# Selecting per-head decays with strips of 32 rows, and applying them to products that two heads share

## The chip, the cores and the metric

The kernel runs on one core of one Trainium2 chip. The metric is device time in microseconds (us) for one execution, the median of three runs. The core has a matrix engine (TensorE, PE in the profile; its weight loads stand apart as PEld), a vector engine (VectorE, DVE), a scalar engine (ScalarE, ACT), GpSimd (POOL), and DMA queues issued here mostly by SyncE (SP). Matmul results land in PSUM, which this kernel hands out in eight banks of 128 partitions by 512 floats.

## The reference

A four-layer model on 256 latent tokens that read 256 context tokens, width 1024. Layers 0 and 3 mix tokens with a bidirectional state-space scan (SSD), layer 1 with spatial gating, layer 2 with retention; each is followed by a SwiGLU FFN. The change lies in the SSD layers alone. Cut to what matters, for each of 32 heads of 64 channels, in each direction, over chunks of 128 tokens:

```
cum    = cumsum(a)                               # a = dt * A, one number per token and head
y      = (C B^T * exp(cum_i - cum_j), masked) @ v        # within the chunk
y     += (C @ state) * exp(cum)                  # from earlier chunks
state  = state * exp(cum[-1]) + B^T @ (v * exp(cum[-1] - cum))
y_all  = y_forward + y_backward + d_skip * x
```

C and B (128 numbers per token) are common to the eight heads of a group; the decays differ by head. Layer 0 computes 512 tokens (four chunks), layer 3 needs outputs for the 256 latent tokens only, with the context's final states still carried in.

## The kernel before

Channels lie on partitions and tokens along the free dimension. Projections are three matmuls per 128x128 weight tile (`mm3`, L306 to L308): the f32 operands are split into a rounded part and a remainder, declared float32r. A stream of weight tiles comes in over SP's queue and is split two ways, `whi` by ACT (L226) and `wlo` by DVE (L227), three units ahead of use.

The order is written by hand. `run` walks the projection jobs of a group of heads, and after each job emits the next slot from a list made by `scan_slots`. A slot holds steps of head pairs (four pairs for each of four groups, so 16 per SSD layer):

- `T_` transposes a pair's inputs (L998), ACT copies them out (L1000), and DVE weights them four times (L1006) into `vs` and `vo`.
- `V_` forms the context states `S` (L1019); ACT copies and POOL multiplies them (L1023, L1025).
- `A_` broadcasts the cumulative decays `ER` of one head over 128 partitions by a matmul with a selector column of `SEL` (L1041, L1049); DVE multiplies them into each head's own operands: `SO` (L1043, L1051) and `C2` (L1053).
- `K_` does the same with the log decays `FR`, on top of a mask: for each head and direction one bfloat16 matmul `IDB` by `NEG` (L1063) and one selector matmul (L1065) into the same bank. ACT takes 16 exponentials of 128 columns in layer 0, 8 in layer 3 (L1070), and DVE adds directions and multiplies with the scores into `E` (L1071, L1072).
- `Y_` sums, per head and into 64 output partitions, the within-chunk term (`E`), the neighbouring chunk (`SO`) and the carried state (`C2`), all in L1091; DVE adds `d * x` (L1095).

`FR` and `ER` hold 64 rows (direction, head) with rounded parts above and remainders below, made once per layer in `b` of `dt_steps` (emitted as the slot `dtb`), from cumulative sums `p3` of `LA`, which POOL produces (L918). Every `ps()` takes the next of the eight PSUM banks in turn, so the ninth allocation waits for the release of the first. DVE, ACT and POOL execute in emission order.

Of the kernel before, what the change touches and what calls it, by code (L numbers as in the profile page):

```python
# [9 lines left out]
F32 = mybir.dt.float32  # L10
# [102 lines left out]
def backbone(ctx, tc, A, out):  # L113
# [33 lines left out]
    def f32(ap):  # L147
        return ap.bitcast(F32)
# [11 lines left out]
    SEL = cp.tile([P, 64], F32R, name="SEL")  # L160
# [642 lines left out]
    def ssd(i, j, need_ctx, prev_last, prev_ranges, norms, fin_norms):  # L803
# [5 lines left out]
        with ExitStack() as ph:  # L809
# [18 lines left out]
            def prep():  # L828
# [5 lines left out]
                if i == 0:  # L834
                    act.copy(IDB, ident)
                    for d, m in ((0, M_GT), (1, M_LT)):
                        dve.tensor_scalar(NEG[d], m, -2.0 ** 100, None, op0=MUL)
                    act.copy(SEL, CST[:, C_SEL:C_SEL + 64])

# [43 lines left out]
            ER = qt([NTOK], "er", dt=F32R)  # L883
# [3 lines left out]
            def dt_steps():  # L887
# [34 lines left out]
                def b():  # L922
# [16 lines left out]
                    act.copy(FR[:64], p3[:64])  # L939
                    dve.tensor_tensor(FR[64:], p3[:64], f32(FR[:64]), op=SUB)  # L940
                    ef = tmp(512, "th", 2)[:64]
                    act.activation(ef, p3[:64], AF.Exp)
                    act.copy(ER[:64], ef)
                    dve.tensor_tensor(ER[64:], ef, f32(ER[:64]), op=SUB)
# [16 lines left out]
            def scan_slots(g):  # L961
# [26 lines left out]
                def pair(hp):  # L988
# [42 lines left out]
                    def sel(d_, h):  # L1031
                        return SEL[:, 32 * d_ + h:32 * d_ + h + 1].to_broadcast([P, P])

                    def A_():
                        pst["C2"] = qt([2, 2, T], "C2", c2)
                        SO = pst["SO"] = qt([2 * W // T, T], "SO", 2)
                        if need_ctx:
                            pt = ps("g")
                            for hh in range(2):
                                for d_ in range(2):  # L1040
                                    pe.matmul(pt[:, (2 * hh + d_) * P:(2 * hh + d_ + 1) * P], sel(d_, h0 + hh),  # L1041
                                              ER[:, (1 - d_) * P:(2 - d_) * P], start=True, stop=True)
                            dve.tensor_tensor(  # L1043
                                SO[:, 0:2], pt.rearrange("p (h n) -> p h n", h=2),
                                st["SF"][:, 0:1].to_broadcast([P, 2, T]), op=MUL)
                        for hh in range(2):
                            pt = ps("g")
                            for d_ in range(2):
                                pe.matmul(pt[:, d_ * T:(d_ + 1) * T], sel(d_, h0 + hh), ER[:, T:],  # L1049
                                          start=True, stop=True)  # L1050
                            dve.tensor_tensor(SO[:, 2 * W // T - 2 + hh], pt[:, P:3 * P], st["SF"][:, W // T - 1], op=MUL)  # L1051
                            C2 = pst["C2"][:, hh]
                            dve.tensor_tensor(  # L1053
                                C2, pt.rearrange("p (d n) -> p d n", d=2),
                                Cg[:, T:].unsqueeze(1).to_broadcast([P, 2, T]), op=MUL)

                    def K_():
                        for hh in range(2):
                            h = h0 + hh
                            pts = [ps("g") for _ in range(2 * W // 512)]  # L1060
# [836 lines left out]
```

## Time and profile before

| | us |
|---|---|
| median of 3 runs (range) | 2883.96 (2882.82 to 2887.27) |
| the profiled execution | 2887.09 |
| its span in the trace | 2885.3 |
| scan of layer 0, in the trace | about 91 to 484 |
| scan of layer 3, in the trace | about 2395 to 2651 |

Times in the trace count from the start of the span. A row of the timeline gives a start, a length and the merged instructions; matmul lengths include the pipeline's drain, so what one costs in a stream is read from the distance between starts. A float32 matmul appears as two instructions (two passes), a float32r or bfloat16 one as one instruction.

### The profile page before, as it was taken

How to read it: one execution, taken by the hardware profiler on the slowest of the kernel's cores; microseconds unless marked ns; L12 is line 12 of the kernel's file. 1: busy time of each engine (PE TensorE's matmuls, PEld its weight loads, DVE VectorE, ACT ScalarE, POOL GpSimd, SP SyncE). 2: the span in 40 equal slices, each digit the busy share in tenths (PEclk: the TensorE clock that was granted, in tenths of full speed). 3: DMA queues.
4: the chain of work that ended last, by engine and by line, in shares of the span. 5: the costliest groups of instructions: out<-in, count | busy, mean ns of one | idle time of the engine just before them, and what ended most of it. 6: DMA issues, size and time to landing. Idle time of an engine off the chain costs nothing.

```text
span 2885.3 us, 40761 instructions
## 1 busy us (share of the span) xinstructions
PE 2822.3 (98%) x16180; PEld 2392.1 (83%) x16180; DVE 1926.2 (67%) x3150; ACT 1092.8 (38%) x1935; POOL 220.7 (8%) x294
## 2 busy tenths in 40 slices
PE   7999999999999999999999999999999999999998
PEld 5787877888889888988889777779888898888998
DVE  5876767678875266677777344346777779888565
ACT  4455444322224422422224322224322245554443
POOL 0210001200001000100001000001000022101000
PEclk9999999999999999999999999999999999999899
DMA  6322233255543222355443222213555422223454
GB/s 235 107 88 103 88 110 118 103 192 195 197 182 110 95 81 88 114 189 174 174 175 118 80 73 88 77 70 110 184 181 176 172 90 99 100 97 118 151 177 140
DMA packets 111678, 376.37 MB, mean 130 GB/s; under 512 B 12160, under 2 KB 16640, under 8 KB 111488
## 3 DMA queue, kind: packets, MB, share of 16 engines
q1 hardware_dynamic: 109296, 367.23, 36.1%
q0 software_dynamic: 1616, 5.77, 0.6%
q8 instruction: 127, 2.08, 0.3%
q10 hardware_dynamic: 576, 0.77, 0.1%
q14 instruction: 63, 0.52, 0.1%
HBM read 369.53 MB, written 4.19 MB: 130 GB/s over the span
## 4 chain that ended last, share of the span: by engine, by line
PE 83%; DVE 6%; issue 6%; ACT 3%; POOL 2%; DMA 0%; POOLq 0%; DVEq 0%; ACTq 0%; SPq 0%
PE mm L306 24%; PE mm L308 24%; PE mm L307 24%; PE y L1091 2%; DVE wlo L227 1%; PE s L1019 1%; PE g L1448 1%; PE g L1063 1%; PE g L1065 1%; DVE AL L577 1%; ACT whi L226 0%; PE y L1312 0%; PE y L1466 0%; PE y L1465 0%; PE s L500 0%
## 5 line engine op out<-in xcount | busy, mean ns | idle before, releaser
L306 PE MATMUL mm<-AH,whi 128*128 128x512 f32 (+1 forms) x2456 | 889.4, 362 | 2.0 <-ACT AH L590 1.6
L308 PE MATMUL mm<-AH,wlo 128*128 128x512 f32 (+1 forms) x2456 | 878.7, 358 | 0.0
L307 PE MATMUL mm<-AL,whi 128*128 128x512 f32 (+1 forms) x2456 | 876.3, 357 | 0.6 <-DVE AL L1120 0.4
L227 DVE TENSOR_TENSOR wlo<-st,whi 128x1024 fp32r<-128x1024 f32 (+1 forms) x502 | 588.7, 1177 | 317.2 <-ACT whi L226 316.9
L226 ACT CAST whi<-st 128x1024 fp32r<-128x1024 f32 (+1 forms) x502 | 503.7, 1008 | 345.9 <-PE mm L307 216.1
L306 PEld LDWEIGHTS mm<-AH,whi 128*128 128x128 f32 x2456 | 463.3, 189 | 74.4 <-issue 3.6
L307 PEld LDWEIGHTS mm<-AL,whi 128*128 128x128 f32 x2456 | 462.9, 188 | 71.3 <-issue 1.2
L308 PEld LDWEIGHTS mm<-AH,wlo 128*128 128x128 f32 x2456 | 462.7, 188 | 71.5
L412 DVE SCALAR_TENSOR_TENSOR mj<-mst,cb 128x1024 bf16<-128x1024 f32 x304 | 371.2, 1221 | 21.8 <-DMA mst<-in_mod_w_dram 16.3
L611 DVE SCALAR_TENSOR_TENSOR X<-mm,MOD,X 128x256 f32<-128x256 f32 x332 | 148.0, 478 | 95.2 <-PE mm L308 95.0
L306 PE MATMUL mm<-hh,whi 128*128 128x512 f32 (+1 forms) x576 | 209.0, 363 | 0.0
L308 PE MATMUL mm<-hh,wlo 128*128 128x512 f32 (+1 forms) x576 | 209.0, 363 | 0.0
L307 PE MATMUL mm<-hl,whi 128*128 128x512 f32 (+1 forms) x576 | 208.8, 363 | 0.0
L306 PE MATMUL mm<-yg,whi 128*128 128x256 f32 (+1 forms) x592 | 198.5, 335 | 1.0 <-ACT yg L1502 1.0
L307 PE MATMUL mm<-yg,whi 128*128 128x256 f32 (+1 forms) x592 | 191.6, 324 | 0.3 <-DVE yg L1503 0.3
L308 PE MATMUL mm<-yg,wlo 128*128 128x256 f32 (+1 forms) x592 | 191.6, 324 | 0.0
L1591 ACT CAST hh<-s 128x512 fp32r<-128x512 f32 (+1 forms) x72 | 40.8, 567 | 288.5 <-DVE s L1581 288.5
L1581 DVE TENSOR_TENSOR s<-s,mm 128x512 f32<-128x512 f32 (+1 forms) x88 | 54.5, 619 | 124.8 <-PE mm L308 124.8
L1563 ACT ACTIVATE s<-mm 128x512 f32<-128x512 f32 (+1 forms) x88 | 47.9, 544 | 210.8 <-PE mm L308 210.7
L308 PEld LDWEIGHTS mm<-hh,wlo 128*128 128x128 f32 x576 | 108.7, 189 | 17.0
L306 PEld LDWEIGHTS mm<-yg,whi 128*128 128x128 f32 x592 | 112.6, 190 | 12.3 <-issue 1.5
L307 PEld LDWEIGHTS mm<-hl,whi 128*128 128x128 f32 x576 | 108.7, 189 | 16.9
(366 smaller groups left out, 3907.9 us busy)
## 6 DMA issues: line engine op xcount, KB each, us to landing
st<-in_ffn_w_dram SPq DMA_DIRECT2D x176, 512.0 KB, 3.3
mst<-in_mod_w_dram SPq DMA_DIRECT2D x152, 512.0 KB, 4.2
st<-in_ssd_in_dram SPq DMA_DIRECT2D x82, 512.0 KB, 3.3
st<-in_ffn_w2a_dram SPq DMA_DIRECT2D x96, 384.0 KB, 3.0
st<-in_ssd_out_dram SPq DMA_DIRECT2D x32, 512.0 KB, 3.3
st<-in_ret_in_dram SPq DMA_DIRECT2D x32, 512.0 KB, 3.3
st<-in_mod_n_dram SPq DMA_DIRECT2D x24, 512.0 KB, 4.1
st<-in_ffn_w2b_dram SPq DMA_DIRECT2D x16, 512.0 KB, 3.8
```

Source lines behind the costliest of these rows:

```text
L226: act.copy(hi[:, :n], t[:, :n])
L227: dve.tensor_tensor(lo[:, :n], t[:, :n], f32(hi[:, :n]), op=SUB)
L306: pe.matmul(pt, lh, rh, start=(start and i == 0), stop=False)
L307: pe.matmul(pt, lh, rl, start=False, stop=False)
L308: pe.matmul(pt, ll, rh, start=False, stop=(stop and i == n - 1))
L412: dve.scalar_tensor_tensor(j, t, 1.0, mp[1][:, v], op0=MUL, op1=MUL, accum_out=MOD[:, i, v, ct:ct + 1])
L577: dve.scalar_tensor_tensor(AL[:, m, n0:n1], u, sh, f32(AH[:, m, n0:n1]), op0=ADD, op1=SUB)
L611: dve.scalar_tensor_tensor(X[:, m, a:b], pt[:, a - n0:b - n0], g, X[:, m, a:b], op0=MUL, op1=ADD)
L1091: pe.matmul(pt[hs, c * P:(c + 1) * P], l_, r_, start=first[hh], stop=(n_ == len(seq) - 1))
L1563: act.activation(t[:, :b - a], pt, AF.Silu)
L1581: dve.tensor_tensor(s, s, pt, op=MUL)
L1591: act.copy(hh[:, a:b], s)
```

## The change

1. `SEL` shrinks to 16 columns with the same pattern in each strip of 32 rows; a sign column `SGN` marks the rows of remainders.
2. `FR` and `ER` are laid out as four strips of 32 rows: strip 2*direction + head parity, 16 rows of rounded parts and 16 of remainders. For that, DVE copies `LA` into a reordered `la` before the `p3` matmuls, which become 16 instead of 8.
3. `K_` issues the four mask matmuls first, then the four selector matmuls, each of 32 rows by 128 columns in a strip of its own.
4. `A_` selects with tiles of 32 rows by 64 columns, in float32; `er[d]` holds both heads' decays in their 64 partitions each. Beside it `gd[d]` holds both heads' products of state with C and of `vo` with `SF`, 128 wide. ACT copies `er` out, DVE multiplies, POOL adds the directions, and DVE adds `d * x`.
5. `Y_` keeps the within-chunk term only. `SO` and `C2` as operands are gone.
6. `A_` moves from the slot ahead of `K_` to the slot of `K_` behind it (layer 0) or the slot after it (layer 3); `V_` moves with the slots.

```
-    SEL = cp.tile([P, 64], F32R, name="SEL")
+    SEL = cp.tile([P, 16], F32R, name="SEL")
+    SGN = cp.tile([P, 3], F32, name="SGN")
...
+                    la = tmp(512, "th", 2)
+                    dve.tensor_copy(la.rearrange("p (c b k h) -> p c b k h", c=8, b=2, k=2),
+                                    LA.rearrange("p c (d h b) -> p (c d) b h", d=2, b=2).unsqueeze(3)
+                                    .to_broadcast([P, 8, 2, 2, 16]))
                     for k in range(4):
-                        for d_, m in ((0, M_LE), (1, M_GE)):
-                            pe.matmul(p3[32 * d_:32 * d_ + 32, k * P:(k + 1) * P],
-                                      LA[:, k, 32 * d_:32 * d_ + 32], m, start=True, stop=True)
+                        for z, m in enumerate((M_LE, M_LE, M_GE, M_GE)):
+                            pe.matmul(p3[32 * z:32 * z + 32, k * P:(k + 1) * P],
+                                      la[:, P * k + 32 * z:P * k + 32 * z + 32], m, start=True, stop=True)
...
-                    act.copy(FR[:64], p3[:64])
-                    dve.tensor_tensor(FR[64:], p3[:64], f32(FR[:64]), op=SUB)
...
+                    def parts(out, x, t):
+                        act.copy(out, x)
+                        dve.tensor_scalar(t, x, SGN[:, 0:1], None, op0=MUL)
+                        dve.scalar_tensor_tensor(out, f32(out), SGN[:, 1:2], t, op0=MUL, op1=ADD)
+                    parts(FR, p3, tmp(512, "th", 2))
...
                     def A_():
...
+                        o = P if need_ctx else 0
+                        er = [ps("g") for _ in range(2)]
+                        gd = [ps("g") for _ in range(2)]
+                        for a, b, n in (((0, o, P),) if need_ctx else ()) + ((o, o + T, T),):
+                            for d_ in range(2):
+                                c = T if n == T else (1 - d_) * P
+                                for hh in range(2):
+                                    pe.matmul(er[d_][64 * hh:64 * hh + 64, a:b], f32(sel(d_, h0 + hh, 64)),
+                                              ER[rows(d_, h0 + hh), c:c + n], start=True, stop=True)
+                        S, vo, SF = pst["S"], pst["vo"], st["SF"]
+                        for d_ in range(2):
+                            ks = slice(d_ * P, (d_ + 1) * P)
+                            seq = [(o + k * P, S[:, d_, k ^ d_], Cg[:, (2 + k) * P:(3 + k) * P]) for k in range(2)]
+                            seq.append((o + (1 - d_) * P, vo[:, d_, 1], SF[:, W // T - 1, ks]))
+                            if need_ctx:
+                                seq.append((0, vo[:, d_, 0], SF[:, 0, ks]))
+                            for n_, (a, l_, r_) in enumerate(seq):
+                                pe.matmul(gd[d_][:, a:a + P], l_, r_, start=(n_ == 0), stop=(n_ == len(seq) - 1))
+                        U = qt([W], "SO", 2)
+                        ec = qt([3 * T + 2 * o], "C2", c2)
+                        L = ec[:, 2 * (o + T):]
+                        x = XT[ct]
+                        for d_ in range(2):
+                            out = U[:, W - T:] if d_ == 0 else L
+                            sc = ec[:, d_ * (o + T):(d_ + 1) * (o + T)]
+                            act.copy(sc, er[d_][:, :o + T])
+                            if need_ctx and d_ == 0:
+                                dve.tensor_tensor(U[:, P:], gd[0][:, :P + T], sc[:, :P + T], op=MUL)
+                                continue
+                            if need_ctx:
+                                dve.tensor_tensor(U[:, :P], gd[1][:, :P], sc[:, :P], op=MUL)
+                            dve.tensor_tensor(out, gd[d_][:, o:o + T], sc[:, o:o + T], op=MUL)
+                        pool.tensor_tensor(U[:, W - T:], U[:, W - T:], L, op=ADD)
+                        dve.scalar_tensor_tensor(
+                            x[:, lo:], x[:, lo:], prm("ssd_d", j * 16 + ct), U, op0=MUL, op1=ADD)
...
                     def K_():
...
+                                gs[d_, hh] = ps("g")[:, :W]
+                                pe.matmul(gs[d_, hh], IDB, NEG[d_].unsqueeze(1).to_broadcast([P, 4 - c0, P]),
+                                          start=True, stop=False)
+                        for hh in range(2):
+                            for d_ in range(2):
+                                pe.matmul(gs[d_, hh], sel(d_, h0 + hh, P), FR[rows(d_, h0 + hh), lo:],
+                                          start=False, stop=True)
...
-                        dve.scalar_tensor_tensor(
-                            x[:, lo:], x[:, lo:], prm("ssd_d", j * 16 + ct), pt[:, lo:], op0=MUL, op1=ADD)
+                        dve.tensor_tensor(x[:, lo:], pt[:, lo:], x[:, lo:], op=ADD)
...
                 if need_ctx:
                     return [
-                        [init, TT[0]], [AA[0], VV[0]], [KK[0], TT[1]],
-                        [YY[0], AA[1], VV[1]], [KK[1], TT[2]],
-                        [YY[1], AA[2], VV[2]], [KK[2], TT[3]],
-                        [YY[2], AA[3], VV[3]], [KK[3]], [YY[3]]]
+                        [init, TT[0]], [VV[0]], [KK[0], AA[0], TT[1]],
+                        [YY[0], VV[1]], [KK[1], AA[1], TT[2]],
+                        [YY[1], VV[2]], [KK[2], AA[2], TT[3]],
+                        [YY[2], VV[3]], [KK[3], AA[3]], [YY[3]]]
 
                 return [
-                    [init, TT[0]], [AA[0]], [VV[0], KK[0], TT[1]], [AA[1]],
-                    [YY[0], VV[1], KK[1], TT[2]], [AA[2]], [YY[1], VV[2], KK[2], TT[3]], [AA[3]],
-                    [YY[2], VV[3], KK[3]], [], [YY[3]]]
+                    [init, TT[0]], [VV[0]], [KK[0], TT[1]], [AA[0], VV[1]],
+                    [YY[0], KK[1], TT[2]], [AA[1], VV[2]], [YY[1], KK[2], TT[3]], [AA[2], VV[3]],
+                    [YY[2], KK[3]], [AA[3]], [YY[3]]]
```

## Rows read from the trace of the kernel before

**Rows 1.** The page: busy time by engine; the chain that ended last.

```profile
PE 2822.3 (98%) x16180; PEld 2392.1 (83%) x16180; DVE 1926.2 (67%) x3150; ACT 1092.8 (38%) x1935; POOL 220.7 (8%) x294
...
PE 83%; DVE 6%; issue 6%; ACT 3%; POOL 2%; DMA 0%; POOLq 0%; DVEq 0%; ACTq 0%; SPq 0%
```

**Rows 2.** Busy time in the two scans: stretch, length, PE, PEld, DVE, ACT, POOL, clock.

```profile
91.00:484.00 393.00, 388.28 (x2611) 310.27 (x2612) 283.35 (x434) 198.68 (x482) 35.39 (x48) 1.00 0.28 96
2395.00:2651.00 256.00, 253.12 (x2019) 228.22 (x2020) 224.78 (x416) 139.91 (x317) 28.90 (x49) 0.99 0.27 93
```

**Rows 3.** Timeline of PE, layer 0, 186 to 199: start, length, engine, line, operation.

```profile
186.62 1.07 PE L422 MATMUL y<-st,CC 128*32 128x256 f32 x16
187.62 0.50 PE L306 MATMUL mm<-yg,whi 128*128 128x512 f32 x1
...
190.51 0.56 PE L1041 MATMUL g<-er,SEL 128*128 128x128 f32 x4
190.91 0.68 PE L1049 MATMUL g<-er,SEL 128*128 128x256 f32 x4
191.43 1.05 PE L1019 MATMUL s<-vps,btok 128*128 128x128 f32 x8
...
197.80 0.39 PE L1063 MATMUL g<-NEG,IDB 128*128 128x512 bf16 x1
...
198.27 0.39 PE L1063 MATMUL g<-NEG,IDB 128*128 128x512 bf16 x1
```

**Rows 4.** Timeline, layer 0, 118 to 122: the pair's `Y_` between its neighbours.

```profile
118.06 0.39 PE L307 MATMUL mm<-AL,whi 128*128 128x512 f32 x1
...
118.29 0.40 PE L308 MATMUL mm<-AH,wlo 128*128 128x512 f32 x1
...
118.61 1.09 PE L1091 MATMUL y<-E,xtok 128*64 128x128 f32 x16
...
119.54 1.04 PE L1091 MATMUL y<-SO,vpo 128*64 128x128 f32 x16
...
121.38 0.66 PE L1041 MATMUL g<-er,SEL 128*128 128x128 f32 x4
```

**Rows 5.** Timeline of PE, layer 3, 2481 to 2485.

```profile
2481.97 0.61 PE L1091 MATMUL y<-SO,vpo 128*64 128x128 f32 x8
...
2483.38 1.16 PE L1019 MATMUL s<-vps,btok 128*128 128x128 f32 x8
2484.38 0.27 PE L1063 MATMUL g<-NEG,IDB 128*128 128x256 bf16 x1
...
2484.61 0.28 PE L1063 MATMUL g<-NEG,IDB 128*128 128x256 bf16 x1
```

**Rows 6.** Costliest groups, shapes apart: count, busy us, mean ns, idle before.

```profile
L1053 DVE TENSOR_TENSOR C<-g,ct 128x512 f32<-128x512 f32 x64 | 43.4, 678 | 0.0
...
L1196 POOL TENSOR_TENSOR X<-X,AH 128x256 f32<-128x256 f32 x12 | 8.8, 749 | 15.1 <-DVE X L1195 15.1
```

**Rows 7.** Timeline, layer 0, at `dtb`: PE's sums and DVE's queue.

```profile
92.75 1.07 PE L933 MATMUL g<-CST,SF 128*32 128x128 f32 x16
...
93.26 0.67 DVE L1144 SCALAR_TENSOR_TENSOR zt<-zt,mm 128x512 f32<-128x512 f32 x1
```

**Rows 8.** Timeline, layer 3, at `dtb`: the same two.

```profile
2398.81 1.92 PE L933 MATMUL g<-CST,SF 128*32 128x128 f32 x16
...
2399.98 0.41 DVE L1144 SCALAR_TENSOR_TENSOR zt<-zt,mm 128x256 f32<-128x256 f32 x1
```

**Rows 9.** Timeline, end of layer 0's scan: idle before, and what ended it, in brackets.

```profile
464.33 0.75 DVE L1006 TENSOR_TENSOR vps<-xtok,ws 128x256 f32<-128x256 f32 x2
464.56 1.06 PE L1091 MATMUL y<-E,xtok 128*64 128x128 f32 x13 [1.62 <-DVE E L1072]
...
475.32 4.23 ACT L1070 ACTIVATE E<-g,bi 128x128 f32<-128x128 f32 x16
...
481.14 0.95 PE L1091 MATMUL y<-E,xtok 128*64 128x128 f32 x13 [1.66 <-DVE E L1072]
```

More of the change, by code (lines that the diff above doesn't have):

```diff
@@ L837, in prep @@
                         dve.tensor_scalar(NEG[d], m, -2.0 ** 100, None, op0=MUL)
-                    act.copy(SEL, CST[:, C_SEL:C_SEL + 64])
+                    q32 = ident.rearrange("p (b q) -> p q b", q=32)
+                    s32 = tmp(32, "s32", 1)
+                    dve.tensor_reduce(s32, q32, axis=mybir.AxisListType.X, op=ADD)
+                    dve.tensor_tensor(SEL[:, :16], s32[:, :16], s32[:, 16:], op=ADD)
+                    dve.tensor_reduce(SGN[:, :1], s32[:, 16:], axis=mybir.AxisListType.X, op=ADD)
+                    for k in (1, 2):
+                        dve.tensor_scalar(SGN[:, k:k + 1], SGN[:, :1], float(k - 3), 1.0, op0=MUL, op1=ADD)
             def conv_evac(ct, dst):
@@ L882, in ssd @@
             FR = qt([NTOK], "fr", dt=F32R)
-            ER = qt([NTOK], "er", dt=F32R)
+            ER = qt([NTOK], "er")
             LN = qt([4, 64], "SD")
@@ L1029, in V_, with rows @@
                                 op=MUL)
-                    def sel(d_, h):
-                        return SEL[:, 32 * d_ + h:32 * d_ + h + 1].to_broadcast([P, P])
-                    def A_():
[L1035 to L1045, printed above, removed]
+                    def rows(d_, h):
+                        z = 2 * d_ + h % 2
+                        return slice(32 * z, 32 * z + 32)
@@ new lines, in sel @@
+                    def sel(d_, h, n):
+                        return SEL[rows(d_, h), h // 2:h // 2 + 1].to_broadcast([32, n])
+                    def A_():
+                        o = P if need_ctx else 0
[33 more added lines that the diff above has]
+                            x[:, lo:], x[:, lo:], prm("ssd_d", j * 16 + ct), U, op0=MUL, op1=ADD)
@@ L1046, in A_, with K_ @@
+                    def K_():
+                        gs = {}
                         for hh in range(2):
-                            pt = ps("g")
                             for d_ in range(2):
[L1049 to L1052, printed above, removed]
@@ L1058, in K_ @@
                         for hh in range(2):
                             h = h0 + hh
-                            pts = [ps("g") for _ in range(2 * W // 512)]
-                            gs = [pts[d_ * W // 512][:, d_ * W % 512:d_ * W % 512 + W] for d_ in range(2)]
-                            for d_ in range(2):
-                                pe.matmul(gs[d_], IDB, NEG[d_].unsqueeze(1).to_broadcast([P, 4 - c0, P]),
-                                          start=True, stop=False)
-                                pe.matmul(gs[d_], sel(d_, h), FR[:, lo:], start=False, stop=True)
```

33 lines of the change are left out of this document (8 added, 25 removed).

## The prediction

> **What bounds the kernel now.** I read the page first: TensorE is busy 98% of the span, and the chain that ended last lies on it for 83%, on VectorE for 6% [rows 1]. So a microsecond taken from TensorE's stream should come off the end, unless it comes back as a wait. Next the windows of the two scans, the only places that the change touches: TensorE is busy 388 of 393 us in layer 0 and 253 of 256 us in layer 3, at full clock or within 1% of it; VectorE stands at 72% in layer 0 but at 88% in layer 3 [rows 2]. In layer 0 VectorE has room, in layer 3 it is the next limit. Since matmul lengths contain the drain, I price TensorE by distances between starts in the timeline. There is little slack to win beside the stream itself: where TensorE waits, it waits for `E` at the end of layer 0's scan [rows 9].
>
> **Prices read from the stream.** A 512-column projection matmul starts 0.23 us after the one before it (118.06 to 118.29) [rows 4]. A change from full-width matmuls to 64-column tiles delays the first by about 0.1 us (118.29 to 118.61 is 0.32 instead of 0.23) [rows 4]; I charge 0.1 us for each entry and exit of a tile shape. Tiles do run side by side: sixteen 256-column passes in four strips of 32 output columns take 1.00 us up to the next projection [rows 3], so 0.80 us without entry and exit, about 0.21 us for four passes at once. In `Y_`, sixteen 128-column passes in two strips take 0.93 us [rows 4], twice as fast as the eight full-width passes of `V_` in 0.80 us [rows 3]. What no row shows is strips of rows, which read different partitions and write different banks. Its bounds: four at the price of one, as the column strips do, or one after another. I take four at once, by the column strips as the nearest row.
>
> **Layer 0, for each of 16 pairs.** Removed: the selectors of `A_`, 0.92 us (190.51 to 191.43) [rows 3]; `K_`, four masks and four selectors at 0.47 us a pair (197.80 to 198.27), 1.88 us [rows 3]; of `Y_` the operands `SO` and `C2`, 1.84 us from 119.54 to 121.38 [rows 4], less the exit of 0.1 us, which stays: 1.74 us. Together 4.54 us. Added: four masks at half of 0.47 us, 0.94 us; four selectors at once, one 512-column stream of 0.23 us, with entry 0.1 us; the `er` selectors, two passes of 256 columns and two of 128 four at a time, 0.21 + 0.21 + 0.11 + 0.11 = 0.64 us, with entry and exit 0.2 us; the common products, eight float32 matmuls at 0.2 us from `V_` (eight passes, four matmuls, in 0.80 us) [rows 3], 1.60 us, or 1.80 us by layer 3's `V_` at 1.00 us [rows 5]; I take 1.75 us. Together 3.86 us. The balance is -0.68 us a pair, -10.9 us for the layer. The common products save nothing by themselves: 1.75 us replaces 1.74 us, because two 64-column strips already ran side by side. The gain is the selectors under the masks.
>
> **Layer 3, for each of 16 pairs.** Removed: four 256-column selectors, at most the 0.52 us of layer 0's (190.91 to 191.43) [rows 3]; `K_`, four times 0.23 us, 0.92 us [rows 5]; `SO` and `C2`, 1.41 us (2481.97 to 2483.38) less 0.1 us, 1.31 us [rows 5]. Together 2.75 us. Added: masks 4 x 0.115 = 0.46 us, selectors 0.115 us with entry and exit 0.2 us, `er` 0.42 us with 0.2 us, six common products at 0.22 us, 1.32 us. Together 2.72 us: nothing is won here. TensorE's stream gives -11 us in all.
>
> The Trainium skill, TensorEngine Tiling (Array Packing), Key Properties, says that a change of tiling mode drains TensorE; this speaks against a change that adds such changes to every pair. The trace agrees that there is a price, 0.1 us at the entry above, and that price is in the sum. The skill's TensorE: Matmul & The Clock Gate, Part 3, gives 3.07 times for four row strips of 512 columns. By that estimate the selector stream of layer 0 would be four times 0.23 us over 3.07, or 0.30 us instead of 0.23 us, some 1 us less gain over the layer. No row here shows it.
>
> **What the `la` copy costs.** `p3` now waits for a copy on VectorE, whose queue at that point ends with the last projection's `zt` (L1144). In layer 0 that ends at 93.93, while TensorE reaches `p3` at 92.75 [rows 7]. A 512-wide VectorE operation takes 0.68 us [rows 6], so `p3` starts near 94.7: 1.9 us late. In layer 3 `zt` ends at 2400.39, the copy near 2401.1, against 2398.81 [rows 8]: 2.3 us late. Everything of that group stands behind it in TensorE's order. The `p3` matmuls double, but run in four strips instead of two, at no cost. Bounds: 1.2 us a layer if the copy cost nothing, 3 us if the clock is low when it ends (the sixteen passes took 1.92 us in layer 3 against 1.07 us in layer 0 [rows 7, 8]). I take +4 us for both.
>
> **Waits that move.** VectorE's evacuations from PSUM cost 0.68 us for 512 columns [rows 6]. In layer 0 the multiplies of a pair shrink from 2048 columns and `d * x` to 768 columns, `d * x`, and a 512-wide add: about 1.0 us less. In layer 3 they shrink from 1536 and `d * x` to 512, `d * x`, and a 256-wide add: 1.0 us less as well. Against that, `d * x` now waits behind POOL's addition, 0.75 us for 256 columns [rows 6] and more if POOL is busy. VectorE stands still meanwhile, with the next pair's `vs` and weight remainders `wlo` queued behind it. ACT has two `er` copies between the exponentials and the transposed input's copy. So `vs`, which came right behind `E` [rows 9], comes about 3 us later (the multiplies 1.0 us, POOL 0.75 us, `d * x` 0.7 us, the hand-overs), and `V_` on TensorE needs it one slot on. On the credit side TensorE does `A_` between `K_` and `Y_`, so `Y_` is reached about 2 us later after its `K_`, and the two waits of 1.6 us for `E` at the end of layer 0 vanish [rows 9]. I set -3 us for these two, and +5 us for new waits of `V_` for `vs`: where projections are few (in layer 0's last group `vs` began at 464.33, so now near 467.5, while TensorE comes to `V_` near 465.5: 2 to 3 us) and in layer 3's first slots of each group. Bounds: +0 if the moved slots cover them, +16 us if half of all pairs wait a microsecond. The nine banks of a slot with `K_`, `A_` and `T_` I price at nothing: `T_` reuses the first mask's bank, free after four of the sixteen exponentials (4.23 us together [rows 9]), while `A_` keeps TensorE busy 2.6 us; without that cover it would cost about 1 us a pair.
>
> **The sum.** -11 + 4 - 3 + 5 = -5 us. The profiled execution took 2887.1 us (span 2885.3 us), 3.1 us above the median of 2883.96 us; -5 us makes it 2882 and the median 2879 us. A difference under 0.2%, 5.8 us, can't be told from no change here, so the forecast sits at that border.
>
> **Rivals.**
>
> - Strips of rows run one after another, so the change doesn't do what it says. For: no row shows row strips. Against: column strips overlap fully [rows 3]. Layer 0 would pay 3 x 0.23 us for the masks' selectors and 3 x 0.64 us for `er`, layer 3 3 x 0.115 and 3 x 0.42 us: 4.2 us for a pair in each layer, +67 us, 2946 us. Chance 0.07. Overlap in twos: a third of it, +22 us, 2901 us. Chance 0.09.
> - VectorE becomes the limit of layer 3. For: 88% busy [rows 2], and each pair adds a wait for POOL of 0.75 us or more and one for the `er` copies. Against: a microsecond of multiplies goes. It decides once the two waits pass the saved 1.0 us by more than the idle 12% of 16 us a pair, 1.9 us. Beyond that point each microsecond is one on the end; a microsecond for 12 pairs turns -5 into +7 us, 2891 us. Chance 0.15.
> - The waits cost nothing: `V_` finds `vs` ready, since VectorE's queue is shorter by 32 us in both scans. Then -5 us becomes -10 us, 2874 us. Chance 0.17.
> - The forecast, 2879 us, 2873 to 2885 us. Chance 0.52.
>
> **How the numbers follow.** Faster by over 0.2% (below 2878.2 us): all of the fourth case and somewhat under half of the forecast, 0.40. Slower by over 0.2%: both strip rivals and most of the third, 0.28. Between: 0.32. The range runs from 2867 us (TensorE's full 11 us and the waits for `E`, with a little of `la` given back) to 2898 us, which leaves out the serial strips, most of those in twos, and little at the low end.
>
> **What would show it.** The four selectors of `K_` start within about 0.03 us of each other and the next tile shape follows some 0.3 us later; if they start 0.23 us apart, the first rival holds. `p3` starts 1.9 and 2.3 us behind the sums before it with VectorE's copy as releaser. `Y_` at the end of layer 0 waits for nothing; `V_` waits for `vs`. POOL's addition shows as a releaser of VectorE of about 1 us per pair. Wrong it would be if row strips overlap badly, if the slots' new order makes `V_` or the projections wait for VectorE in every pair, or if an idle stretch lowers the clock, which no term holds.

## The result, and the profile after

The changed kernel takes 2936.39 us (median of 4 runs, 2933.07 to 2941.6) against 2885.61 us of the kernel before beside it: ratio 1.0172, 95% interval [1.016, 1.0184]. It is slower by 1.7%, outside the range of the prediction.

The page after, span and busy times, against [rows 1]:

```profile
span 2932.1 us, 40495 instructions
...
PE 2856.4 (97%) x15956; PEld 2374.5 (81%) x15956; DVE 1913.2 (65%) x3127; ACT 1116.5 (38%) x1996; POOL 242.1 (8%) x326
```

TensorE has 224 instructions fewer and is busy 34 us longer. The windows of the two scans, against [rows 2]:

```profile
91.00:485.00 394.00, 389.40 (x2505) 299.27 (x2504) 272.57 (x418) 212.28 (x513) 46.68 (x63) 0.99 0.28 96
2422.50:2700.00 277.50, 264.85 (x1925) 225.66 (x1926) 219.64 (x403) 150.16 (x348) 38.49 (x64) 0.98 0.26 86
```

Layer 0's scan is as long as before. Layer 3's window, which runs 2 us past its scan, is 277.5 us long instead of 256, although VectorE's share fell to 79%: TensorE stands still for 12.6 us in it (277.50 less 264.85), before for 2.9 us. And the scan begins 27 us later (`dtb`'s sums at 2423.5 instead of 2396.0), after layers in which the diff touches nothing. Counted from `dtb`'s first sum to the instruction behind the last `Y_`, as scans are from here on, layer 0 takes 392.7 us in both kernels and layer 3 takes 274.3 instead of 254.8 us. The span is 46.8 us longer: 0 in layer 0, about +28 in the untouched layers, +19 in layer 3, 0 behind it.

A pair of layer 0 on TensorE's timeline, the strips that no row of before could show:

```profile
199.83 1.04 PE L1097 MATMUL g<-NEG,IDB 128*128 128x512 bf16 x4
200.80 0.51 PE L1101 MATMUL g<-fr,SEL 32*128 32x512 f32 x4
201.24 0.88 PE L1063 MATMUL g<-er,SEL 32*64 32x128 f32 x16
202.05 0.71 PE L1073 MATMUL g<-ct,S 128*128 128x128 f32 x4
...
203.94 0.60 PE L1013 MATMUL s<-CST,xs 128*128 128x128 f32 x4
```

Starts give 0.97 us for the masks, 0.44 for four selectors with entry and exit, 0.81 for `er`, 1.89 for the common products: 4.11 us, where the prediction had 3.86. In the trace's single records the four selectors start at 200.800, 200.804, 200.807 and 200.810 and last 0.50 us each: the four row strips do run side by side. (`ER`, unlike what point 2 of the change says, holds whole float32 values in 16 rows of a strip and zeros in the other 16, so its selectors are float32, in two passes.) The Trainium skill's factor of 3.07 (TensorE: Matmul & The Clock Gate, Part 3), with which the prediction had an estimate of 0.30 us beside 0.23 us, lies as close to these 0.44 us as full overlap does: entry and exit are not told apart finely enough here.

TensorE's waits in layer 3's scan (2420 to 2700), in total, times and longest:

```profile
PE s L1034 <- DVE vps L1021: 7.4, 3, 2.6
PE y L935 <- POOL SF L926: 4.1, 1, 4.1
PE g L946 <- DVE th L941: 2.0, 1, 2.0
PE g L1097 <- ACT C L1081: 1.7, 1, 1.7
```

The second was there before. The others are new: `V_` for `vs` three times, `p3` for `la`, a mask for a bank. Behind the scan there is one more, 1.7 us at the first projection that reads the normalised `AH` (L307, released by ACT's L1145). On VectorE, POOL's addition holds up `d * x` by 0.86 us a pair in both layers, as forecast:

```profile
DVE xs L1089 <- POOL SO L1088: 27.5, 32, 0.9
```

The sums at `dtb` in layer 3 on PE and DVE, against [rows 8]:

```profile
2425.35 1.06 PE L937 MATMUL g<-SF,CST 128*128 128x256 f32 x2
2428.39 1.08 PE L946 MATMUL g<-CST,th 128*32 128x128 f32 x32 [1.99 <-DVE th L941]
```

```profile
2427.50 0.41 DVE L1170 SCALAR_TENSOR_TENSOR zt<-zt,mm 128x256 f32<-128x256 f32 x1
2427.83 0.42 DVE L941 COPY th<-SF 128x512 f32<-128x512 f32 x1
```

`p3` waits behind `zt` and the copy, 1.99 us (in layer 0, against [rows 7], 1.14 us); the copy takes 0.42 us where the prediction had 0.68. At the end of layer 0's scan, against [rows 9], `Y_` indeed waits no more; `V_` waits 0.57 us at 470.81.

### The profile page after: what moved, and what is told of

Its sections match the earlier page's. It is cut to its first block, busy times and chain, and to the rows that moved or that the text cites. A ratio compares the mean times of both kernels' runs of the same rounds, so it can differ in the third digit from the quotient of the medians.

```text
span 2932.1 us, 40495 instructions
## 1 busy us (share of the span) xinstructions
PE 2856.4 (97%) x15956; PEld 2374.5 (81%) x15956; DVE 1913.2 (65%) x3127; ACT 1116.5 (38%) x1996; POOL 242.1 (8%) x326
## 5 line engine op out<-in xcount | busy, mean ns | idle before, releaser
L307 PE MATMUL mm<-AH,whi 128*128 128x512 f32 (+1 forms) x2456 | 897.4, 365 | 3.2 <-ACT AH L1145 1.7
L308 PE MATMUL mm<-AL,whi 128*128 128x512 f32 (+1 forms) x2456 | 886.2, 361 | 0.6 <-DVE AL L1146 0.4
L307 PEld LDWEIGHTS mm<-AH,whi 128*128 128x128 f32 x2456 | 463.9, 189 | 84.8 <-issue 3.3
L307 PE MATMUL mm<-hh,whi 128*128 128x512 f32 (+1 forms) x576 | 211.0, 366 | 0.0
L307 PE MATMUL mm<-yg,whi 128*128 128x256 f32 (+1 forms) x592 | 200.2, 338 | 1.0 <-ACT yg L1528 1.0
L307 PEld LDWEIGHTS mm<-hh,whi 128*128 128x128 f32 x576 | 108.4, 188 | 19.2
```

The lines of the kernel that those rows point to most:

```text
L307: pe.matmul(pt, lh, rh, start=(start and i == 0), stop=False)
L308: pe.matmul(pt, lh, rl, start=False, stop=False)
```

## What the untouched layers lose

The same matmuls take longer. Groups of TensorE by form, mean in ns behind the comma: the normalised activations and the FFN's hidden tiles as moving operands, first before, then after.

```profile
L307 PE MATMUL mm<-AL,whi 128*128 128x512 f32 x1696 | 662.1, 390 | 0.0
...
L307 PE MATMUL mm<-hl,whi 128*128 128x512 f32 x432 | 168.1, 389 | 0.0
```

```profile
L308 PE MATMUL mm<-AL,whi 128*128 128x512 f32 x1696 | 670.8, 396 | 0.0
...
L308 PE MATMUL mm<-hl,whi 128*128 128x512 f32 x432 | 170.5, 395 | 0.0
```

From start to start, 228.0 ns becomes 233.3 ns for the first and 226.7 becomes 232.6 for the second, at the full clock. What differs is where tiles lie. `SEL` shrank from 256 to 64 bytes per partition, `SGN` was added in 32, a new small tile `s32` takes 128: in the allocation of the compiled programs `whi` and `wlo` start 160 bytes lower than before, the hidden tiles 32 lower. `AH` and `AL`, allocated ahead of `SEL`, stay. The kernel before has pads among its tiles already (`PAD_W`, `PAD_H`), so it too stood at chosen places.

## The experiments

**Place** (e1 to e4 beside a kernel before of 2888.01 us). Theory: the changed kernel's 27 to 28 us in untouched layers come from the tiles' starts, no longer multiples of 64 bytes; rival: from the change's work. e1 is the changed kernel with the old starts:

```
-    SGN = cp.tile([P, 3], F32, name="SGN")
+    SGN = cp.tile([P, 48], F32, name="SGN")
...
-                    s32 = tmp(32, "s32", 1)
+                    s32 = tmp(512, "th", 2)[:, :32]
```

> The changed kernel with SGN widened to 48 columns and s32 taken from an existing buffer, so that every tile behind SEL stands at the address it had before the change; no instruction differs otherwise. Theory P (placement): the 32-byte offset that the two smaller tiles gave all later tiles slows each 512-column matmul by about 5 ns, also in layers that the change does not touch. Then the stretch from the end of layer 0's scan to layer 3's, 27 us longer in the changed kernel, goes back to its old length, some 4 us come back in each scan, and the time is about 2902 us (2895 to 2910), with the spacing of 512-column matmuls back at 226 to 230 ns. Theory W (waits): the loss comes from the new waits in the scans alone; then the time stays at 2936 us within 5.

Measured 2910.77 us, 1.0081 [1.0068, 1.0095]: 25.6 us less than the changed kernel, 0.8 us above the expected range, and layer 3's `dtb` starts 0.8 us from where it did before the change. e2 and e3 give the kernel before an unused tile of 8 or 16 floats behind `SEL`:

```
     SEL = cp.tile([P, 64], F32R, name="SEL")
+    cp.tile([P, 8], F32, name="SHIFT")
```

> The kernel before, with an unused tile of 8 floats (32 bytes) behind SEL and nothing else changed. Theory P: placement alone slows the untouched layers; the spacing of 512-column matmuls goes from 226-230 to 231-234 ns and the time to about 2918 us (2910 to 2926). Theory W: no instruction differs, so 2885 us within 4.

Measured 2906.17 us, 1.0065 [1.0051, 1.0079]: slower with not one instruction of the computation changed, and 4 us below the range expected.

> The kernel before, with an unused tile of 16 floats (64 bytes) behind SEL. If what counts is whether a tile starts at a multiple of 64 bytes, the time stays at 2885 us within 4; if any move from the old addresses costs, 2900 us or more. Theory W: 2885 us.

Measured 2877.0 us, 0.9964 [0.995, 0.9977]: faster than before, which no multiple-of-64 rule foresaw.

e4 has strips in `K_` alone, with `la` on VectorE; `A_`, `Y_` and the slots are those before, starts too.

```
+                        for z, m in enumerate((M_LE, M_LE, M_GE, M_GE)):
+                            pe.matmul(p3[32 * z:32 * z + 32, k * P:(k + 1) * P],
+                                      la[:, P * k + 32 * z:P * k + 32 * z + 32], m, start=True, stop=True)
...
+                        for hh in range(2):
+                            for d_ in range(2):
+                                pe.matmul(gs[d_, hh], *strip(d_, h0 + hh), start=False, stop=True)
```

> One part alone, at the old addresses: FR and ER in strips of 32 rows (with the la copy on VectorE), the four selector matmuls of K_ one strip each; A_, Y_ and the slots as before the change, with full-height selectors in A_. Sum of the prediction for these parts: -0.7 us a pair in layer 0 and about 0 in layer 3, +4 us for the two waits for la: about 2878 us (2873 to 2884). If strips of rows brought nothing on TensorE: 2889 us or more. Under theory W's stronger form (strips themselves cause lasting waits): above 2895 us.

Measured 2896.73 us, 1.003 [1.0019, 1.0041], far above the 2873 to 2884 us expected and in the range of theory W's stronger form: layer 0's scan +1 us, layer 3's +11, -2 behind it. TensorE's waits in layer 0's scan, and then in layer 3's:

```profile
PE y L1114 <- DVE E L1095: 6.7, 5, 1.7
...
PE g L944 <- DVE th L939: 1.5, 1, 1.5
```

```profile
PE g L944 <- DVE th L939: 2.2, 1, 2.2
...
PE s L1011 <- DVE ct L860: 1.4, 1, 1.4
PE g L1082 <- ACT S L1036: 1.4, 3, 0.9
PE g L1082 <- DVE X L1187: 1.2, 2, 0.6
```

In layer 0 `K_` takes 22.4 us from start to start instead of 29.5: strips alone save 7.0 us on TensorE. All of it comes back: 4.7 us are waits (`Y_` 6.7 us for `E` instead of 4.5, because a shorter `K_` covers less of the exponentials, `p3` 1.5 us, the projections 1.0 for `wlo`), 3.4 us more of the scan are at the half clock, and some 2 us are not traced. That the gain needs the move of `A_` behind `K_` is argued from the 2.2 us of `Y_`, not shown. In layer 3 `K_` now takes four banks instead of two and its masks (L1082) wait 2.6 us for the bank's last reader, `p3` and a transpose (L1011) wait too, and 17 us of the scan are at the half clock instead of 5.

**Place, another rule** (e12, like e9 to e11, beside a kernel before of 2887.55 us). e3 asked for another rule; e12 shifts the kernel before by 48 floats, so that all starts remain multiples of 64 bytes.

```
-    cp.tile([P, 16], F32, name="SHIFT")
+    cp.tile([P, 48], F32, name="SHIFT")
```

> The kernel before with an unused tile of 48 floats behind SEL, so that every later tile starts 192 bytes further on. All starts stay multiples of 64 bytes. Theory 64 (what costs time is a start that is no multiple of 64 bytes): no slower than the kernel before, 2877 to 2888 us. Theory R (what counts is where moving and stationary tile start relative to each other, modulo 256 bytes: 227 ns for 512 columns where they start alike, 228 ns at 64 bytes apart, 233 at 32 or 96 or 160 apart, as the hidden layers, which moved together, show): whi and wlo then stand 128 bytes from AH and AL, which don't move, where the changed kernel's hh and whi, 128 apart, took 232.6 ns; 4,900 such matmuls by 5 ns make +20 to +25 us, 2903 to 2910 us, while the matmuls from hh and hl keep 227 ns.

Measured 2906.15 us, 1.0062 [1.0048, 1.0076]. Theory R's number came, the multiple-of-64 theory is out. The same two groups in e12, then in e3:

```profile
L308 PE MATMUL mm<-AL,whi 128*128 128x512 f32 x1696 | 669.5, 395 | 0.0
L308 PE MATMUL mm<-hl,whi 128*128 128x512 f32 x432 | 168.1, 389 | 0.0
```

```profile
L308 PE MATMUL mm<-AL,whi 128*128 128x512 f32 x1696 | 660.3, 389 | 0.0
L308 PE MATMUL mm<-hl,whi 128*128 128x512 f32 x432 | 168.0, 389 | 0.0
```

Mean distances of starts (ns; 512 columns but for the last matmul), worked out from the traces, with how far the weight tile's start lies from the other operand's, modulo 256 bytes, from the allocation:

```
                        before   after     e2      e3      e12
AL moving, whi          228.0    233.3    233.2   227.2   232.8
AH moving, whi          230.0    233.3    233.4   226.9   232.7
AH moving, wlo          229.5    233.3    233.3   227.0   232.8
  apart (bytes)           192       32      224       0      128
hl moving, whi          226.7    232.6    226.8   226.9   226.9
  apart (bytes)             0      128        0       0        0
whi moving, AL          233.2    233.4    233.2   226.4   232.6
AL, whi, 256 columns    117.4    118.4    116.7   119.8   118.7
  apart (bytes)           192       32      224       0      128
```

All pairings of 512 columns in the table take 226 to 227 ns where both tiles start alike modulo 256 bytes, and 232 to 233 ns otherwise, but for 228 to 230 ns with `AL` or `AH` moving in the kernel before. The 5,088 matmuls of three products by 1,696 with `AH` and `AL` moving take 229.2 ns in the mean of the kernel before, 233.3 in e2 and 232.8 in e12: 21 and 18 us, where 18.2 and 18.6 us were measured. At 256 columns the order is the other way round:

```profile
L307 PE MATMUL mm<-AL,whi 128*128 128x256 f32 x760 | 214.2, 282 | 0.6 <-DVE AL L1120 0.4 <-POOL AL L591 0.2
```

```profile
L308 PE MATMUL mm<-AL,whi 128*128 128x256 f32 x760 | 216.4, 285 | 0.6 <-DVE AL L1121 0.3 <-POOL AL L592 0.2
```

That is the kernel before and then e3, whose starts are alike; `hl` with `whi`, too, takes 119.9 ns alike and 118.6 at 128 bytes apart (the changed kernel). In e3 the 2,280 such matmuls of three products by 760 give back 5 of the 16 us that the longer ones gain, which leaves the 10 to 11 us measured.

Two things stay open. 256 is the theory's own modulus: tiles that start alike here do so modulo 512 bytes as well, and no run separates the two. Distances of 96 and 160 bytes, which the expectation names, were not run. What in the chip makes it so was not tried.

**Layer 3's waits** (e5 to e8 beside a kernel before of 2886.98 us). e1 still loses 22 us in layer 3's scan (276.8 us against 254.8). e5 moves the later `V_` of a group back, behind `T_` by two slots:

```
-                    [init, TT[0]], [VV[0]], [KK[0], TT[1]], [AA[0], VV[1]],
-                    [YY[0], KK[1], TT[2]], [AA[1], VV[2]], [YY[1], KK[2], TT[3]], [AA[2], VV[3]],
+                    [init, TT[0]], [VV[0]], [KK[0], TT[1]], [AA[0]],
+                    [YY[0], VV[1], KK[1], TT[2]], [AA[1]], [YY[1], VV[2], KK[2], TT[3]], [AA[2]],
```

> The changed kernel at the old addresses (as e1, 2910.8 us), with V_ in layer 3 moved back one slot, behind T_ by two slots as the kernel before had it: [Y0, V1, K1, T2] instead of [A0, V1], [Y0, K1, T2]. Theory W (the scan of layer 3 is longer by 24 us than before because V_ comes one slot too early for vs and each wait of about 2.8 us is followed by a stretch at the half clock): the three waits of 2.77, 2.85 and 2.88 us go (-7.8 us) and three half-clock stretches of 3.4 us, which cost half of their length, go with them (-5 us): 2898 to 2903 us, layer 3's scan +11 to +16 us instead of +24. Rival B (VectorE's queue is the limit of this layer, so a wait taken from V_ shows up at K_, Y_ or the projections): 2908 to 2912 us. Rival K (the four banks of K_ in layer 3 make the waits, V_ is only where they show): V_ waits as long in its new place, 2908 us or more.

Measured 2907.15 us, 1.0068 [1.0056, 1.0081]: theory W failed, below both rivals' numbers but with intervals of e1 and e5 that overlap. The three waits stood unmoved, because they belong to the *first* `V_` of groups two to four, which e5 had left. The queue of VectorE ahead of one of them, in the changed kernel, and TensorE there:

```profile
2500.05 1.23 DVE L228 TENSOR_TENSOR wlo<-st,whi 128x1024 fp32r<-128x1024 f32 x1 [0.21 <-ACT whi L227]
2501.19 0.69 DVE L871 SCALAR_TENSOR_TENSOR xs<-th,xs 128x512 f32<-128x512 f32 x1
2501.84 3.10 DVE L862 SCALAR_TENSOR_TENSOR bt<-mm,cw,bt 128x508 f32<-128x508 f32 x4
2504.85 0.75 DVE L1021 TENSOR_TENSOR vps<-xtok,ws 128x256 f32<-128x256 f32 x2
```

```profile
2502.57 0.28 PE L309 MATMUL mm<-yg,wlo 128*128 128x256 f32 x1
2505.32 2.08 PE L1034 MATMUL s<-vps,btok 128*128 128x128 f32 x8 [2.47 <-DVE vps L1021]
```

`vs` stands behind the four taps of a convolution (3.10 us) of the next group, and one slot of 256-column projections is too short to cover that. The windows before, right behind and after this wait (the clock is third from the end):

```profile
2500.00:2504.90 4.90, 2.84 (x25) 2.64 (x24) 4.74 (x7) 3.57 (x8) 0.00 (x0) 1.00 0.31 107
2505.00:2508.40 3.40, 3.08 (x14) 3.08 (x15) 3.40 (x7) 1.26 (x3) 0.52 (x1) 0.50 0.04 6
2508.50:2515.00 6.50, 6.50 (x59) 5.58 (x59) 3.39 (x8) 5.14 (x15) 0.72 (x2) 1.00 0.46 155
```

For 3.4 us after it the granted clock is 0.50, the 1.2 GHz level, so a wait of 2.5 us can cost up to 1.7 us more. In e1's layer 3 there were four such stretches that the kernel before doesn't have, behind the three waits for `vs` and one of 1.75 us for a bank, and 3.4 us more of one at `dtb`.

e6 makes the copy of `la` on POOL, ahead of `Ln`, with the old starts.

```
-                    dve.tensor_copy(la.rearrange("p (c b k h) -> p c b k h", c=8, b=2, k=2),
+                    pool.tensor_copy(la.rearrange("p (c b k h) -> p c b k h", c=8, b=2, k=2),
```

> The changed kernel at the old addresses (as e1), with the reordering copy of LA on POOL, behind the product that makes LA, instead of on VectorE behind the last projection's zt. If VectorE's queue makes p3 late (the prediction's step), the waits of 1.9 us in layer 0 and 2.6 us in layer 3 go, less what is left of POOL's own copy (an estimate of 1.5 us for 512 columns from POOL's 0.75 us for 256, against the 1.5 us of TensorE between LA and p3): -2.5 to -4 us, and where the wait was followed by a half clock (6.8 us in layer 0, 3.4 us more than before in layer 3) another -3 to -5 us: 2902 to 2907 us. Rival: the copy itself is what p3 waits for, on whichever engine: 2909 to 2912 us.

Measured 2905.92 us, 1.0066 [1.0053, 1.0078], in the theory's range, though the interval overlaps e1's. Layer 0's `p3` waits less (0.35 us idle instead of 1.46), layer 3's as long as before the move (1.99 us). POOL's row there:

```profile
2397.16 0.62 POOL L932 COPY th<-SF 128x512 f32<-128x512 f32 x1 [3.37 <-DVE xs L871]
```

POOL waited for VectorE to read the buffer `th` that `la` takes (`xs`, L871, from 2396.33 to 2397.02). So neither the engine that copies nor the copy's length sets the wait, but the ring of buffers, and through it VectorE's queue once more, which releases the buffer late.

e7 is e5 and e6 together, 64 bytes further on (`SGN` as `[P, 64]`).

> e5 and e6 together, and every later tile 64 bytes further on, as in e3. If the three causes are independent, their differences add: 2910.8 us - 8 to -13 (V_) - 4 to -8 (la) - 11 (place) = 2879 to 2888 us; against the kernel before at the same place (e3, 2877.0 us) the change then still loses 2 to 11 us. If placement only matters for the kernel before, 2890 to 2899 us.

Measured 2894.32 us, 1.0024 [1.0015, 1.0033], 6 us above the expected sum and inside the rival's range. `V_`'s part of the sum, as e5 shows, never came: with the differences that e5 and e6 measured, -3.6 and -4.9 us, it gives 2891 us. And place does count for the changed kernel: between the two scans e7 takes 1900.8 us, e5 and e6 1914.6 and 1913.9. e9 then moves the first `V_`:

```
-                    [init, TT[0]], [VV[0]], [KK[0], TT[1]], [AA[0]],
+                    [init, TT[0]], [], [VV[0], KK[0], TT[1]], [AA[0]],
```

> e7 (2894.3 us) with the first V_ of each group in layer 3 moved into the slot of the first K_, two slots behind its T_: [], [V0, K0, T1] in place of [V0], [K0, T1]. In e7 TensorE still waits 2.91, 2.85 and 2.64 us at three places, all of them this first V_ of groups two to four, and two stretches of 3.4 us at the half clock follow. Theory W0 (vs of a group's first pair is late because VectorE first finishes the group before, and one slot of projections is too short a cover): the three waits and both stretches go, -7.7 and -3.4 us: 2883 us, within 3. Rival B (VectorE's queue is full there, so the wait turns up at the next thing that needs VectorE): 2891 to 2895 us.

Measured 2886.54 us, 0.9996 [0.9987, 1.0004]: -7.8 us, just short of the 2883 us within 3 that theory W0 had, and clear of the rival. In e7 the waits of layer 3's scan had the line

```profile
PE s L1033 <- DVE vps L1020: 7.6, 3, 2.6
```

and in e9 there is no such line. The only new one is 0.8 us for a transpose, and `p3` waits 2.6 us instead of 2.0. By the two traces the scan is 8.1 us shorter: 5.9 us less of waits, and 5.3 us less at the half clock, of which half is 2.7. Most of the wait did not move on to another user of VectorE: that rival (a full VectorE) falls.

e10 puts layer 3's common products of both directions into halves of one bank.

```
+                        gd = [ps("g") for _ in range(2)] if need_ctx else [ps("g")] * 2
+                        gd = gd if need_ctx else [gd[0][:, :T], gd[0][:, T:]]
```

> e9, and the products of both directions in layer 3 (256 columns each) in halves of one PSUM bank instead of two banks. Before the change a pair of layer 3 took 6 banks (Y, V, K two, T, and two in A_ make 7), changed it takes 11 (Y, V, four in K_, four in A_, T), so K_ and T_ come back to a bank that the exponentials or multiplies still read. In e7 these waits are, by the starts of TensorE, some 2.4 us in front of transposes, 2.5 us in K_ and 1.2 us in A_. Theory K (turning of the banks): a third to a half of it goes, -2 to -3 us against e9. Rival (the waits are for the engines that read, not for the number of banks): within 1 us of e9.

Measured 2884.76 us, 0.9992 [0.9984, 1.0001]. The intervals of e9 and e10 overlap, with medians 1.8 us apart: undecided. e11 gives `la` a buffer that is free.

```
-                    la = tmp(512, "th", 2)
+                    la = qt([512], "E", 2)
```

> e10, with la in a buffer of the E ring, which is free at that time, instead of the th ring. In e6 and e7 POOL stood 3.4 us before the copy in layer 3, released by VectorE's last read of the buffer (xs, L871), and p3 waited 2.6 us as with the copy on VectorE: the buffer, not the engine, made it late. Theory: the copy starts as soon as POOL is free, p3 waits under 1 us in both layers: -2 us for layer 3's wait, -0.5 us for layer 0's, and up to -3 us of half clock behind it: 3 to 5 us below e10. Rival (POOL has other work or the copy itself takes as long): within 1 us of e10.

Measured 2881.45 us, 0.9978 [0.9969, 0.9986]: -3.3 us, the size expected. The intervals overlap by 0.0002, but the 11 runs of each, on one chip, differ by 3.6 us in the mean (95% interval 1.5 to 5.7). POOL and TensorE at layer 3's `dtb` in e11:

```profile
2382.41 0.64 POOL L932 COPY E<-SF 128x512 f32<-128x512 f32 x1
```

```profile
2383.45 1.06 PE L941 MATMUL g<-SF,CST 128*128 128x256 f32 x2
2384.44 1.20 PE L945 MATMUL g<-CST,E 128*32 128x128 f32 x32
```

`p3` follows the sums at once.

**Layer 0 alone.** e8 keeps layer 3 as before and has the change in layer 0, `la` on POOL, 64 bytes further on.

```
+    SEL64 = cp.tile([P, 64], F32R, name="SEL64")
+    SGN = SMALL[:, 8:11]
...
+                    if not need_ctx:
+                        return T_, V_, A3_, K3_, Y3_
```

> The change in layer 0 alone, with la on POOL; layer 3 as the kernel before has it (whole selectors, SO and C2); tiles 64 bytes further on, as in e3. Theory (matmul stream as summed, -11 us in layer 0, of which waits gave back 10): without the la wait and its half clock layer 0 is 4 to 6 us shorter than before, layer 3 +-0, place -11 us: 2871 to 2875 us, 2 to 6 us below e3. Rival (what TensorE saves in layer 0 is lost to VectorE, whatever the order): 2877 us or more, as e3.

Measured 2873.14 us, 0.9949 [0.9937, 0.9962], which can't be told from e3's 0.9964. So e3 ran again as e16 on one chip with e13 to e15 (kernel before 2887.15 us). e13 is e8 with e11's buffer for `la`:

> e8 (the change in layer 0 alone, 64 bytes further on) with la in a buffer of the E ring. If waits give layer 0's saving back, the wait of p3 (1.5 us from start to start) goes, and with it some of the 6.8 us at the half clock behind it: 1 to 4 us below e8, 2869 to 2872 us, 3 to 6 us below e16. If the saving isn't there beside the projections: within 1 us of e8 and e16.

Measured 2871.69 us, 0.9949 [0.9936, 0.9961]. e14 also orders the products by when `S` comes:

```
+                            seq = [(o + (1 - d_) * P, vo[:, d_, 1], SF[:, W // T - 1, ks])]
+                            if need_ctx:
+                                seq.append((0, vo[:, d_, 0], SF[:, 0, ks]))
+                            seq += [(o + k * P, S[:, d_, k ^ d_], Cg[:, (2 + k) * P:(3 + k) * P]) for k in (d_, 1 - d_)]
```

> e13 with the common products in another order: those of vo first, then the two from S that ACT alone makes, and the ones that POOL has multiplied last. In e8 TensorE waits 2.2 and 1.2 us for S in the last pair of layer 0, where no projections are left. Theory: 1 to 2 us of these go, 2867 to 2871 us. Rival (ACT's copy of S is itself late, the multiply of POOL isn't what counts): as e13.

Measured 2870.63 us, 0.9947 [0.9934, 0.9961]: 1.1 us below e13, which fits both and decides nothing. The trace does. TensorE in layer 0's last group, and ACT before it:

```profile
455.34 0.71 PE L1089 MATMUL g<-SF,vpo 128*128 128x128 f32 x4 [1.89 <-ACT nsq L429]
...
457.38 1.22 PE L1089 MATMUL g<-SF,vpo 128*128 128x128 f32 x4 [0.88 <-ACT E L1125]
```

```profile
453.98 1.04 ACT L228 CAST whi<-st 128x1024 fp32r<-128x1024 f32 x1 [2.38 <-DMA st<-in_ssd_out_dram]
454.93 0.37 ACT L429 COPY nsq<-y 128x256 f32<-128x256 f32 x1
```

The products wait with `vo` in front as with `S`. By the profile's releasers they wait for ACT's read of another result (`nsq`) and for its first exponentials (4 from 456.19, of 4.24 us for 16): it is the turn of the PSUM banks, not `S`. And ACT's read is itself late: it stands behind a cast of `whi` that waited 2.38 us for a weight tile's DMA. No run takes that wait away.

e15 has both layers:

> The whole change with all repairs (e11, 2881.5 us) and the order of e14 in both layers. Layer 3's stream of K_, A_ and Y_ stays longer than before by some 4 us (in e11 56.3 us against 52.3), which no order mends: 2879 to 2881 us, 8 to 12 us above e14. If what is left of layer 3 were waits for S, it would come within 5 us of e14.

Measured 2882.84 us, 0.9984 [0.9975, 0.9993], as e11 and 12 us above e14: what layer 3 still loses is not a wait for `S`.

> e3 once more, in one call with the three above, so that they can be compared on one chip: ratio to the kernel before 0.995 to 0.998 as there, 2874 to 2880 us.

Measured 2876.73 us (2876.33 to 2876.95), 0.9965 [0.9953, 0.9978], as e3. All runs of e13 (2869.55 to 2873.62) and of e14 (2869.22 to 2874.37) lie below all of e16: layer 0's part is worth 5 to 6 us at the same place. Layer 0's scan takes 393.0 us in e3 and 394.2 in e16, but 388.5 in e13 and 387.4 in e14. One window of the same length over it, in e16 and then in e14, has 81 instructions and 3.3 us less of TensorE:

```profile
88.00:492.00 404.00, 398.36 (x2662) 319.86 (x2662) 291.39 (x445) 203.68 (x487) 37.23 (x50) 0.99 0.28 95
```

```profile
88.00:492.00 404.00, 395.04 (x2581) 307.92 (x2582) 285.74 (x440) 217.69 (x520) 53.34 (x69) 1.00 0.30 98
```

e13 and e14 are the best versions: 0.5% under the kernel before, of which about 10 us are place and 5 to 6 us the change.

## Why the prediction was wrong

- **The step that failed** is "the two scans, the only places that the change touches" and with it the sum, which has no term outside of them. The change also moved tiles, and 512-column matmuls then took 233 ns from start to start instead of 227 to 230. By e1 this is 25.6 of the 50.8 us; e2 and e12 make 18 to 19 us of it without any change of work.
- **"TensorE's stream gives -11 us in all"** was mis-sized. Layer 0's added part costs 4.11 us a pair instead of 3.86 us: -0.43 us a pair, -7 us. In layer 3, put at nothing, `K_`, `A_` and `Y_` of a pair that doesn't wait take 3.39 us in e11 against 3.33 in the kernel before (medians of 16 pairs), so the sum of these terms was right to 1 us. (The 56.3 against 52.3 us of e15's expectation don't come out of the traces: to the end of the last pair it is 56.9 against 55.0 us, 1.6 and 0.8 of them waits.) Yet at the same place, with as much waiting (2.0 and 2.4 us) and half clock (3.2 and 3.1 us), layer 3's scan takes 260.1 us in e11 and 255.2 in e3: +4.9 us, of which the three steps are 1.4, the transposes 1.4 and the projections 2.1. The first projection behind `A_` is followed after 0.20 us, where it was 0.12: a price that the sum doesn't have. So about -2 us instead of -11.
- **Strips of rows** overlap as forecast, and both strip rivals are out. The change's gain in layer 0 is real: e13 and e14 show 5 to 6 us.
- **"+4 us for both" for `la`** had the size (1.1 and 2.0 us idle, and a stretch of half clock that was in the bounds), but half the cause: with the copy taken off VectorE (e6) layer 3 waited as long, for the buffer that VectorE was still to read. e11 brought 3.3 us back.
- **"+5 us for new waits of `V_`"** had the place, "layer 3's first slots of each group", and the wrong price there: 7.4 us of waits plus the half clock behind them. e9 recovered 7.8 us for one step moved by one slot.
- **"If an idle stretch lowers the clock, which no term holds"**: it did. The five longest new waits in e1's layer 3, 11.5 us together, have some 17 us more at half clock behind them, which cost up to 8.5 us on top.
- **"The nine banks of a slot I price at nothing"**: the masks and, in layer 0's last group, the common products do wait for banks: 1.7 us in layer 3, 1 to 3 us at 455 to 464 in layer 0, there in part because ACT waits for a weight tile. That `Y_` at the end of layer 0 stops waiting (-3) was right, and these waits take its place.
- **VectorE as the limit of layer 3** is out: with `V_` placed a slot later its waits of 7.6 us vanish and 1.4 us take their place (e9).

In e1 layer 3's scan is 21.9 us longer than in the kernel before (e5's expectation has 24). By the traces it waits 10.0 us more (7.7 us for `V_`, 2.0 for `p3`, 2.3 for banks, less 1.9 that the kernel before waits elsewhere), loses up to 8.5 us to the half clock, and keeps the 4.9 us that are left when waits and clock are as before (e11): 23.4 us at most. The runs bear out `V_` with its clock (e9) and `p3` (e11), while the banks' part stayed within the error (e10), and a change of layer 3's stream alone wasn't run. At the same place the whole change, repaired, is still 6 us slower than the kernel before (e15 and e16, whose runs don't overlap). In their traces layer 0's scan is 6.0 us shorter, layer 3's 4.9 us longer, and what stands behind it 4.2 us longer, where TensorE waits 2.2 us for `AH` and 3.6 us more are at the half clock.

## What to carry to other kernels

Before pricing a change that adds or shrinks a tile, list where every later tile then starts, above all both operands of the matmuls that fill the span: here 160 bytes cost over twice what the change was to save. Look at each width of matmul by itself: the place that was best for 512 columns was the worst for 256. Price a new wait on the bounding engine by what stands ahead in the releasing queue at that slot and by the buffer that the releaser writes into, and a wait of 2.5 us by up to two thirds more for the clock behind it. Where a change serves two layers of different shape, try it in each alone: here one of the two gained.

## What the runs showed of the hardware

- The rate of float32r matmuls depends on where both operands start: 227 ns for 512 columns with starts alike modulo 256 bytes, 232 to 233 ns at 32, 128 or 224 bytes apart. For 256 columns it is 120 ns alike and 117 to 119 ns otherwise. Over this kernel that is 19 us between e12 and the kernel before, and 10 to 11 us gained by e3.
- A wait of 2.5 us can be followed by 3.4 us at a granted clock of 0.50 (windows above), although TensorE then works on without a gap: behind all three waits for `vs` in e1's layer 3 and one of 1.75 us for a bank, behind two of the three for `vs` in e5's.
- Four strips of 32 rows by 512 columns, each into a bank of its own, take 0.44 us with entry and exit (the changed kernel, at 200.80), and sixteen float32 passes of 32 rows by 64 columns 0.81 us.
